# Hybrid encoder layer: the next step's key copies one unit earlier, the output sums behind the first block's low part

## The chip, the cores and the metric

The kernel runs on one core of a Trainium2 chip. Its engines are named as the profile names them: PE is TensorE (PEld is its weight load), DVE is VectorE, ACT is ScalarE, POOL is GpSimd, SP is SyncE, which here only issues DMAs. The metric is the device time of one execution in microseconds (us). Lower is better.

## The reference, cut to what matters

One encoder layer is applied to two sequences of 512 tokens, with model width 1024, all in float32. Attention and a state-space branch read the same normalised input, their gated sum goes through `w_out`, and an MLP follows. The change lies in the attention:

```
s = einsum('nqkgd,njkd->nkgqj', qb, kw) * scale + bias      # query blocks of 128, keys of 3 neighbouring blocks
s = where(mask, s, NEG_INF)
p = softmax(concatenate([s, sink_col]))[..., :-1]
o = einsum('nkgqj,njkd->nqkgd', p, vw)
```

There are 16 query heads of 64, 4 key heads, and 4 query heads share one key head. Queries and keys are RMS-normalised over the 64 elements of a head first. A block of 128 queries sees the key block before it, its own and the one after it, so the first and the last of the four blocks of a sequence see two key blocks and the others three.

## The kernel before, in words

Products are kept close to float32 by splitting operands into a high part (rounded to the matmul's format, made on ACT) and a low part (the rest, made on DVE or POOL).

**Steps and units.** The attention runs over 8 steps (key head j, sequence sq), and each step over 4 units, the query blocks qb = 0 to 3. The order of the work on PE, DVE, ACT and POOL is written out by hand in one loop body, and each engine executes its instructions in that order. SP's queue is ordered by a scheduler. Three things are interleaved in a unit:

- the current block `cur`: `scores(h)` on PE for four heads (L991, into a PSUM tile `sps`, of which there are two), `largest(h)` on DVE (L995, adds the bias and finds the maximum `nmx`; with its accumulator read it frees the `sps` tile), `exp(h)` on ACT (L1001, in place in `p`);
- the block before it, `prev`: `turn(i)` transposes the p of key block i on PE (L1007, into a PSUM tile `tps`, of which there are two), `high(i)` rounds it on ACT (L1011, `ph`), `low(i)` is the rest on DVE (L1016, `pl`), and `value(i, part)` multiplies ph (part 0) or pl (part 1) by the values on PE (L1023). All of a block's value products accumulate in one PSUM tile `po`. The pool of `po` has one buffer, `ps_o` with bufs=1;
- the projection of a query tile of the next step: `project(n)` on PE (L919, `acc`), `square` on ACT (L925, `sq`), `power` on POOL (L932 to L939, `rq`), `norm` on DVE (L943, `qn`), and one unit later `turn` (L952), `high` and `low` (L967, L971, `qa`).

**The output sum.** A value product yields two halves of `po`. At a unit's end ACT copies the lower half (`lower_part`, L1027, `ol`), and in the unit after that DVE adds the two (`owed.add()`, two instructions L1033, each reading `po` and `ol` and writing `ya`). So the sum of block n-2 runs in unit n. In the same unit PE's `value(0, 0)` of block n-1 begins to fill `po` again.

**The key copies.** `key_copies` on POOL (L888) copies the next step's normalised keys twice side by side into `kd`. `key_turn` transposes `kd` on PE (L901, into a `tps` tile), and ACT (L902) and DVE (L903) make `kh` and `kl`, which the next step's scores use. Both happen in the unit qb = 0. `kd` and `qn` share a pool of two buffers.

**Further work.** In units 2 and 3 DVE also multiplies the former step's `ya` by its gate (`late.gated`, L1068) and by the inverse sums (`late.multiply`, L1072). In units 0 and 1 of steps 1 to 4, and in all of steps 0, 6 and 7, ACT and POOL prepare a piece of weights (L873 or L785 on ACT, L874 or L786 on POOL) at a unit's end. Steps 6 and 7 also split the state-space branch's result (L1090 on ACT, L1087 on POOL), and they move the norm into the unit's first half (`prompt`), with a sum over the head on DVE (L936). Step 7 has no next step, so PE fills its gaps with products of the state-space branch (L125).

Lines up to L1180 have the same numbers before and after the change.

Of the kernel before, what the change touches and what calls it, by code (L numbers as in the profile page):

```python
# [33 lines left out]
NB = SEQ // BLOCK  # L34
# [30 lines left out]
def hybrid_layer(ctx, tc, x, x_t, w_kv, rel, onehot, w_qkv, w_ug, vectors, lam, coefs, w_glu, w_out, ln2,  # L65
# [469 lines left out]
    with tc.tile_pool(name="hst", bufs=1) as hp:  # L535
# [11 lines left out]
        with tc.tile_pool(name="ssmt", bufs=2) as sp:  # L547
# [123 lines left out]
            pending = []  # L671
# [166 lines left out]
    with tc.tile_pool(name="att", bufs=2, reuse_waits="tile") as ap, tc.tile_pool(name="attc", bufs=1, reuse_waits="tile") as ac:  # L838
# [17 lines left out]
        steps = [(j, sq) for j in range(N_KV) for sq in range(NSEQ)]  # L856
# [29 lines left out]
        def key_copies(j, sq):  # L886
            kd = ap.tile([P, 4, 2, HD], F32, tag="qn", name="kd")
            GP.tensor_copy(kd, kn[:, sq * 4:sq * 4 + 4, j, None, :].to_broadcast([P, 4, 2, HD]))  # L888
            return kd
# [16 lines left out]
        class Tile:  # L906
# [6 lines left out]
            def project(self, n):  # L913
                (j, sq), col = self.key, self.t * P
                for i in range(self.k, min(self.k + n, 3 * KT)):
                    k, p = divmod(i, 3)
                    hi, lo = weights[j][k // 4]
                    act, w = [(0, hi), (0, lo), (1, hi)][p]
                    PE.matmul(self.ps, hT[sq][act][:, k, col:col + P], w[:, k % 4, :], start=i == 0, stop=i == 3 * KT - 1)  # L919
                self.k += n  # L920
# [186 lines left out]
        def glu_pull(n):  # L1107
            for _ in itertools.islice(early, n):
                pass
# [14 lines left out]
        with tc.manual_schedule(engines={ET.PE, ET.DVE, ET.Activation, ET.Pool}):  # L1124
# [14 lines left out]
            for t in range(4):  # L1139
# [22 lines left out]
                if t == 2:  # L1162
                    kd = key_copies(0, 0)
# [13 lines left out]
                return pending[:2]  # L1177
            return pending[2:]

        pending, y_lows = [], []  # L1180
        prev = owed = lower = turned = None
        with tc.manual_schedule(engines={ET.PE, ET.Activation, ET.DVE, ET.Pool}):
            for i, (j, sq) in enumerate(steps):
                nxt = steps[i + 1] if i + 1 < len(steps) else None
                sums = small.tile([P, G, NB], F32, tag="sm", name="sm", bufs=2)
                ya = ap.tile([P, 2, HALF], F32, tag="ya", name="ya")
                extra = pieces_of(i)
                for qb in range(NB):
                    if 1 <= i < 3:
                        t = (i - 1) * NB + qb  # L1190
                        GP.dma_start(y2_scr[:, :, t, :].rearrange("g c k -> c g k"), y_scr[t])
                    for m in {6: (qb,), 7: ((4, 5, 6, 7), (), (), ())[qb]}.get(i, ()):
                        load_y(m)
                    ready = {6: ((0,), (1,), (2,), (3,)), 7: ((4,), (5, 6), (7,), ())}.get(i, ((),) * 4)[qb]
                    cur = Unit(j, sq, qb, sums, ya)
                    n3 = prev.nkb if prev else 0
                    div = Divide(*steps[i - 1], *done) if qb == 1 and i > 0 else None
                    new = Tile(*nxt, qb) if nxt else None
                    project = new.project if new else lambda n: glu_pull(n // 2)
                    kd, prompt = None, not nxt or (i == 6)  # L1200
                    if rows and not nxt:
                        rows.pt = acc()
                    if rows and not rows.qn:
                        rows.power(halving=not prompt)
                    while y_lows:
                        y_lows.pop(0)()
                    cur.scores(0)
                    cur.largest(0)
                    if i == 7 and qb == 3:
                        final = Divide(j, sq, sums, ya, True)  # L1210
                        final.load_gate(ap, "p", 3)
                    cur.scores(1)
                    if owed:
                        owed.add()
                    cur.largest(1)
                    if n3:
                        prev.turn(0)
                        prev.turn(1)
                        prev.high(0)
                    project(6)  # L1220
                    if n3:
                        prev.low(0)
                    cur.exp(0)
                    cur.exp(1)
                    if rows and not rows.qn and prompt:
                        rows.norm()
                    if qb == 0 and nxt:
                        kd = key_copies(*nxt)
                    if div:
                        div.invert()  # L1230
                    cur.scores(2)
                    cur.largest(2)
                    if n3:
                        prev.high(1)
                    project(4)
                    if n3:
                        prev.value(0, 0)
                    project(2)
                    cur.exp(2)
                    cur.scores(3)  # L1240
                    if lower:
                        lower()
                        lower = None
                    if n3:
                        prev.low(1)
                        prev.value(0, 1)
                    if rows and not rows.qn:
                        rows.norm()
                    cur.largest(3)
                    if n3 > 2:  # L1250
                        prev.turn(2)
                    if rows and prompt:
                        rows.turn()
                    if kd and prompt:
                        key_turn(*nxt, kd)
                    if div:
                        div.turn()
                    project(4)
                    if n3 > 2:
                        prev.high(2)  # L1260
                        prev.low(2)
                    for tile_ in (turned, rows if prompt else None):
                        if tile_:
                            tile_.high()
                            tile_.low()
                    if n3:
                        prev.value(1, 0)
                    if kd and not prompt:
                        key_turn(*nxt, kd)
                    cur.exp(3)  # L1270
                    project(4)
                    if n3:
                        prev.value(1, 1)
                    project(4)
                    turned = None if prompt else rows
                    if turned:
                        rows.turn()
                    if n3 > 2:
                        prev.value(2, 0)
                        prev.value(2, 1)  # L1280
                    if new:
                        new.square()
                    if qb == (2 if nxt else 3) and late:
                        late.gated()
                    if qb == 3 and late and nxt:
                        late.multiply()
                    if n3:
                        prev.lower_part()
                    for m in ready:
                        y_lows += [split_y(m, half) for half in range(2)]  # L1290
                    if extra:
                        lower = extra.pop(0)()
                    if qb == 1:
                        late = div
                    owed, prev, rows = prev, cur, new
                    if nxt and qb == NB - 1 and sq == 1:
                        load_biases(nxt[0])
                done = sums, ya
            owed.add()
            glu_pull(6)  # L1300
            for k in range(prev.nkb):
                prev.turn(k)
                prev.high(k)
                prev.low(k)
                glu_pull(4)
            late.multiply()
            load_gates(0)
            gate_out(0)
            for k in range(prev.nkb):
                prev.value(k, 0)  # L1310
                prev.value(k, 1)
            load_gates(1)
            prev.lower_part()
            prev.add()
            glu_pull(13)
            gate_out(1)
            final.invert()
            final.turn()
            glu_pull(24)
            pieces[2] = glu_pieces(2, cpool, GP)  # L1320
            column_half(2, 0)
            column_half(2, 1)
            final.gated()
            for u in range(2):
                gated_states(u, ap, "qn")
                mixed(u)
            gate_out(2)
            gate_out(3)
            gated_states(2, ap, "qn")
            column_half(3, 0)  # L1330
            column_half(3, 1)
            final.multiply()
# [74 lines left out]
    with tc.tile_pool(name="rn2", bufs=2, reuse_waits="tile") as rn2:  # L1407
# [150 lines left out]
        xb, owed = [], None  # L1558
# [5 lines left out]
        for t in range(NT // 2):  # L1564
# [7 lines left out]
            for sq in range(NSEQ):  # L1572
# [28 lines left out]
                owed = sq, t, norm_of(x1, *scaled)  # L1601
# [280 lines left out]
```

## Time and profile before

| | |
|---|---|
| median of 3 runs | 1445.36 us (1444.78 to 1446.15) |
| the profiled execution | 1444.43 us, of which the span from first to last instruction is 1442.6 us |
| PE busy | 1431.5 us, 99% of the span |
| DVE, ACT, POOL busy | 1097.7, 771.0, 290.6 us |
| granted TensorE clock | 0.999 |
| attention loop | about 432 to 655 us of the span, some 28 us a step |

Busy PE means that matmuls are in flight. Their ends are modelled, and the weight load of the next matmul overlaps the one in flight, so a short stop of PE shows first as idle time ahead of a weight load (PEld). In a row of the timeline stand the start, the duration, the engine, the line, the operation, output<-input and the count; in brackets the idle time ahead of it and what ended it. DVE's next instruction may start a little before the row of the one ahead of it ends.

### The profile page before, as it was taken

The numbers are of one execution on the slowest core, as the hardware profiler recorded it, in microseconds if no ns is written. First come the engines' busy times: TensorE is split into PE (matmuls) and PEld (weight loads), VectorE is DVE, ScalarE is ACT, GpSimd is POOL, SyncE is SP. The second block draws the span as 40 slices with busy tenths as digits, with TensorE's granted clock in tenths as the row PEclk, the third lists the DMA queues.
The fourth block names the chain that finished last, engine by engine and source line by source line (L and its number), as shares of the span: only waits on it lengthen the run. The fifth ranks groups of instructions, "written<-read, shape, count | busy, mean of one in ns | idle before, by whom it ended". The sixth has DMA issues, their size and how long they took to land.

```text
span 1442.6 us, 22132 instructions
## 1 busy us (share of the span) xinstructions
PE 1431.5 (99%) x7941; PEld 1222.5 (85%) x7941; DVE 1097.7 (76%) x1983; ACT 771.0 (53%) x1387; POOL 290.6 (20%) x534
## 2 busy tenths in 40 slices
PE   9999999999999999999999999999999999999998
PEld 7888888889999999887888888888888888888887
DVE  7999959995458999988976588777776597575644
ACT  8688861224348888894543255455544443333332
POOL 3044452004246766463100000000000000000000
PEclk9999999999999999999999999999999999999999
DMA  7356549529641542346552344444442983464341
GB/s 297 102 171 186 177 146 324 206 97 311 224 175 60 166 123 80 119 140 202 182 198 83 132 143 164 161 161 161 147 148 93 364 313 104 147 200 146 120 131 59
DMA packets 102206, 240.24 MB, mean 167 GB/s; under 512 B 12331, under 2 KB 25131, under 8 KB 102097
## 3 DMA queue, kind: packets, MB, share of 16 engines
q1 hardware_dynamic: 62304, 139.94, 29.8%
q0 software_dynamic: 16320, 48.28, 10.1%
q10 hardware_dynamic: 23472, 50.61, 9.5%
q8 instruction: 63, 1.03, 0.3%
q14 instruction: 47, 0.38, 0.1%
HBM read 169.02 MB, written 81.82 MB: 174 GB/s over the span
## 4 chain that ended last, share of the span: by engine, by line
PE 76%; DVE 10%; issue 5%; POOL 3%; ACT 3%; DMA 3%; SPq 0%; DVEq 0%; ACTq 0%; POOLq 0%
PE bank L119 13%; PE bank L120 13%; PE bank L118 13%; PE acc L187 10%; PE acc L125 6%; PE acc L919 3%; PE sps L641 2%; PE sps L753 2%; DVE t L716 2%; PE sps L991 2%; PE acc L120 1%; PE acc L119 1%; PE acc L118 1%; DVE t L718 1%; DVE t L717 1%
## 5 line engine op out<-in xcount | busy, mean ns | idle before, releaser
L187 PE MATMUL acc<-act,c_hi 128*128 128x512 f32 x768 | 243.8, 395 | 0.0
L119 PE MATMUL bank<-b_lo,a_hi 128*128 128x512 f32 (+1 forms) x449 | 174.7, 389 | 0.1
L120 PE MATMUL bank<-b_hi,a_lo 128*128 128x512 f32 (+1 forms) x449 | 174.5, 389 | 0.0
L118 PE MATMUL bank<-b_hi,a_hi 128*128 128x512 f32 (+1 forms) x449 | 174.5, 389 | 0.0
L187 PEld LDWEIGHTS acc<-act,c_hi 128*128 128x128 f32 x768 | 142.3, 188 | 28.0 <-ACT act L316 0.9
L1738 ACT CAST a_hi<-d_a 128x1024 fp32r<-128x1024 f32 x56 | 59.0, 1053 | 178.0 <-PE bank L119 174.7
L187 PE MATMUL acc<-act,c_lo 128*128 128x512 f32 x384 | 151.3, 394 | 0.0
L118 PE MATMUL bank<-act,act 128*128 128x512 f32 x368 | 143.2, 389 | 0.0
L119 PE MATMUL bank<-act,act 128*128 128x512 f32 x368 | 143.2, 389 | 0.0
L120 PE MATMUL bank<-act,act 128*128 128x512 f32 x368 | 143.2, 389 | 0.0
L1739 DVE TENSOR_TENSOR a_lo<-d_a,a_hi 128x1024 fp32r<-128x1024 f32 x56 | 68.5, 1223 | 97.1 <-ACT a_hi L1738 97.1
L919 PE MATMUL acc<-w_hi,act 128*128 128x256 f32 x512 | 113.4, 290 | 0.5 <-DVE qn L943 0.5
L119 PEld LDWEIGHTS bank<-b_lo,a_hi 128*128 128x128 f32 x449 | 84.3, 188 | 18.3 <-DVE b_lo L1739 0.8
L120 PEld LDWEIGHTS bank<-b_hi,a_lo 128*128 128x128 f32 x449 | 84.3, 188 | 17.5
L118 PEld LDWEIGHTS bank<-b_hi,a_hi 128*128 128x128 f32 x449 | 84.3, 188 | 17.4
L919 PEld LDWEIGHTS acc<-w_hi,act 128*128 128x128 f32 x512 | 87.0, 189 | 4.9 <-PE sps L991 0.5
L187 PEld LDWEIGHTS acc<-act,c_lo 128*128 128x128 f32 x384 | 72.2, 188 | 14.6 <-DVE c_lo L178 0.8
L125 PE MATMUL acc<-act,gc_hi 128*128 128x512 f32 x256 | 81.2, 394 | 0.3 <-POOL act L1087 0.3
L119 PEld LDWEIGHTS bank<-act,act 128*128 128x128 f32 x368 | 69.1, 188 | 14.5
L120 PEld LDWEIGHTS bank<-act,act 128*128 128x128 f32 x368 | 69.1, 188 | 14.4
L118 PEld LDWEIGHTS bank<-act,act 128*128 128x128 f32 x368 | 69.1, 188 | 14.2
L1001 ACT ACTIVATE p<-p,nmx 128x257 f32<-128x257 f32 (+1 forms) x128 | 71.8, 563 | 12.9 <-DVE nmx L995 12.0
(370 smaller groups left out, 3467.8 us busy)
## 6 DMA issues: line engine op xcount, KB each, us to landing
d_a<-a_scr SPq DMA_DIRECT2D x56, 512.0 KB, 3.6
raws<-in_w_up_dram SPq DMA_DIRECT2D x32, 512.0 KB, 4.1
a_scr<-t ACTq DMA_DIRECT2D x64, 256.0 KB, 3.0
k<-in_w_down_dram SPq DMA_DIRECT2D x32, 512.0 KB, 6.1
c_raw<-in_w_ug_dram SPq DMA_DIRECT2D x48, 256.0 KB, 3.8
ct_scr<-ctab POOLq DMA_DIRECT2D x16, 512.0 KB, 4.7
ctab_in<-ct_scr POOLq DMA_DIRECT2D x16, 512.0 KB, 6.9
a_scr<-a ACTq DMA_DIRECT2D x32, 256.0 KB, 2.0
```

The source lines that it names most:

```text
L118: PE.matmul(ps, a[0], b[0], start=first, stop=False)
L119: PE.matmul(ps, a[0], b[1], start=False, stop=False)
L120: PE.matmul(ps, a[1], b[0], start=False, stop=last)
L125: PE.matmul(ps, w[wi][:, k, :], rows[yi], start=k + p == 0, stop=k == KT - 1 and p == 2)
L187: PE.matmul(ps, w[wi][:, k, :], hT[s][hi][:, k, :], start=n == 0, stop=n == 3 * KT - 1)
L641: PE.matmul(ps[:, i * P:(i + 1) * P], bm[:, ri, g, :], u_sb[:, gp * SH + g, :], start=True, stop=True)
L716: V.tensor_mul(t1, h[:, i], a8r)
L753: PE.matmul(o, ctab[:, g0 % SI + g, ri, 0:T * CH], st[:, ri, g].rearrange("p s k -> p (s k)"), start=False, stop=ri == 1)
L919: PE.matmul(self.ps, hT[sq][act][:, k, col:col + P], w[:, k % 4, :], start=i == 0, stop=i == 3 * KT - 1)
L1001: S.activation(p, p, AF.Exp, bias=self.nmx[:, h:h + 1], scale=-1.0, accum_out=self.sums[:, h, self.qb:self.qb + 1])
L1738: S.copy(hi, src)
L1739: V.tensor_sub(lo, src, hi.bitcast(F32))
```

## The change

Two edits of the order, no new and no removed instruction. The output sums `owed.add()` move from ahead of `largest(1)` to behind `low(0)` of the block before. The key copies for step i+1, which ran in unit 0 of step i, now run near the end of unit 3 of step i-1, and wait in a list; only the first (made in step 0, for step 1) stays where it was.

```diff
-        pending, y_lows = [], []
+        pending, y_lows, ahead_keys = [], [], []
...
-                    kd, prompt = None, not nxt or (i == 6)
+                    prompt = not nxt or (i == 6)
...
                     cur.scores(1)
-                    if owed:
-                        owed.add()
                     cur.largest(1)
                     if n3:
                         prev.turn(0)
                         prev.turn(1)
                         prev.high(0)
                     project(6)
                     if n3:
                         prev.low(0)
+                    if owed:
+                        owed.add()
                     cur.exp(0)
                     cur.exp(1)
                     if rows and not rows.qn and prompt:
                         rows.norm()
-                    if qb == 0 and nxt:
-                        kd = key_copies(*nxt)
+                    if qb == 0 and i == 0:
+                        ahead_keys.append(key_copies(*nxt))
...
                     if rows and prompt:
                         rows.turn()
+                    kd = ahead_keys.pop() if qb == 0 and nxt else None
                     if kd and prompt:
                         key_turn(*nxt, kd)
...
                     project(4)
+                    if qb == NB - 1 and i + 2 < len(steps):
+                        ahead_keys.append(key_copies(*steps[i + 2]))
                     turned = None if prompt else rows
```

On DVE, in a unit qb = 1 (the instruction that follows is the reciprocal of the sums, L1043), this stood before:

```order
L995 ISA p,nmx<-sps,bias,vec 128x384
L995 ISA nmx 128x1
L1033 TENSOR_TENSOR ya<-po,ol 64x2x128 x2
L995 ISA p,nmx<-sps,bias,vec 128x384
L995 ISA nmx 128x1
L1016 TENSOR_TENSOR pl<-tps,ph 128x512
L1043 RECIPROCAL rsum<-sm 128x16
```

and this stands now:

```order
L995 ISA p,nmx<-sps,bias,vec 128x384
L995 ISA nmx 128x1
L995 ISA p,nmx<-sps,bias,vec 128x384
L995 ISA nmx 128x1
L1016 TENSOR_TENSOR pl<-tps,ph 128x512
L1033 TENSOR_TENSOR ya<-po,ol 64x2x128 x2
L1043 RECIPROCAL rsum<-sm 128x16
```

The two sums moved behind the second `largest` and behind `low(0)`.

On PE nothing moved, but the waits changed. From `value(0, 0)` to `value(0, 1)` of a unit with three key blocks, with the semaphores that each instruction waits for in brackets, before:

```order
L1023 MATMUL po<-ph,va 128x512 [waits DVE_49,Activation_49]
L919 MATMUL acc<-w_lo,act_104 128x256
L919 MATMUL acc<-w_hi,act_105 128x256
L991 MATMUL sps<-kh,qa 128x384 [waits DVE_49]
L991 MATMUL sps<-kl,qa 128x384
L1023 MATMUL po<-pl,va 128x512 [waits DVE_49]
```

and now:

```order
L1023 MATMUL po<-ph,va 128x512 [waits DVE_49,Activation_49]
L919 MATMUL acc<-w_lo,act_104 128x256
L919 MATMUL acc<-w_hi,act_105 128x256
L991 MATMUL sps<-kh,qa 128x384
L991 MATMUL sps<-kl,qa 128x384
L1023 MATMUL po<-pl,va 128x512
```

The waits of `scores(3)` on `largest(1)` and of `value(0, 1)` on `low(0)` are gone: the DVE wait of `value(0, 0)` now covers both.

On POOL, around the start of a step, before:

```order
L939 TENSOR_TENSOR rq<-ms,neg_half 128x4 [waits Pool_49]
L888 COPY kd<-kn 128x512 [waits DVE_49,PE_49]
L1191 DMA y_scr<-y_scr 16x64x128 [waits DMASW5_49]
L983 COPY p<-vec 128x4 [waits DVE_49,PE_49]
L932 TENSOR_TENSOR sq<-sq 128x4x32 [waits Activation_49]
```

and now, one unit earlier:

```order
L939 TENSOR_TENSOR rq<-ms,neg_half 128x4 [waits Pool_49]
L888 COPY kd<-kn 128x512 [waits DVE_49,PE_49]
L1191 DMA y_scr<-y_scr 16x64x128 [waits DMASW4_49]
L983 COPY p<-vec 128x4
L932 TENSOR_TENSOR sq<-sq 128x4x32 [waits Activation_49]
```

The copy moved ahead of one whole chain of `power` (L932 to L939) and of the DMA and the small copy ahead of that chain. On SP one load of the state-space result and the store of a finished `ya` (L1073) change places in step 6, in a queue of which nothing else moves.

## The prediction

> **What bounds the kernel now.** I read the page first, then the stretches of the attention loop and of the stage behind it, then the waits of PE's weight load in the loop.
>
> ```profile
> span 1442.6 us, 22132 instructions
> PE 1431.5 (99%) x7941; PEld 1222.5 (85%) x7941; DVE 1097.7 (76%) x1983; ACT 771.0 (53%) x1387; POOL 290.6 (20%) x534
> ```
>
> ```profile
> 487.00:516.00 29.00, 28.51 (x211) 26.59 (x210) 27.06 (x70) 24.80 (x64) 20.71 (x45) 1.00 0.46 142
> 660.00:680.00 20.00, 20.00 (x90) 16.42 (x90) 18.79 (x24) 7.55 (x14) 5.00 (x5) 1.00 0.65 212
> 720.00:760.00 40.00, 40.00 (x182) 33.19 (x181) 29.39 (x42) 16.89 (x30) 2.68 (x6) 1.00 0.56 195
> ```
>
> ```profile
> PEld po L1023 <- DVE pl L1016: 3.8, 13, 0.3
> PEld tps L901 <- POOL kd L888: 2.5, 4, 0.6
> PEld acc L919 <- POOL w_lo L874: 0.4, 1, 0.4
> ```
>
> PE is the bound: 99% of the span, 28.51 of 29 us in a loop stretch, and all of 20 and 40 us in the stage behind the loop. (Columns of a stretch: its length, PE, PEld, DVE, ACT, POOL busy, the granted clock, DMA.) So a stop taken from PE's order or added to it in the loop passes to the end nearly whole. DVE is close behind in the loop, 27.06 of 29 us. The waits show what the two edits could win at most: 3.8 us for `value` waiting for `pl` (13 times 0.3), 2.5 us for the key transposes waiting for `kd`, 0.4 us for one weight piece behind `kd`.
>
> **The key copies.**
>
> ```profile
> 490.26 0.40 PE L1023 MATMUL po<-ph,va 128*128 128x512 f32 x1
> 490.30 0.60 POOL L888 COPY kd<-kn 128x512 f32<-128x512 f32 x1
> 490.95 0.42 PEld L901 LDWEIGHTS tps<-ident,kd 128*128 128x128 f32 x4 [0.62 <-POOL kd L888]
> 491.37 0.36 PE L919 MATMUL acc<-w_lo,act 128*128 128x256 f32 x1
> 462.28 0.40 PE L1023 MATMUL po<-ph,va 128*128 128x512 f32 x1
> 462.88 0.36 PE L919 MATMUL acc<-w_lo,act 128*128 128x256 f32 x1
> 458.29 1.77 POOL L932 TENSOR_TENSOR sq<-sq 128x128 f32<-128x128 f32 x5 [0.85 <-ACT sq L925]
> ```
>
> From `value(1, 0)` to the projection behind the key transposes PE takes 491.37 - 490.26 = 1.11 us where it waits and 462.88 - 462.28 = 0.60 where it does not: 0.51 us for each of 4 steps, 2.0 us. The copy ends at 490.90 and the load starts at 490.95, so a semaphore costs 0.05. With the weight piece the early copy wins 2.0 + 0.4 = 2.4 us. [...]
>
> Its new place costs nothing: it is 0.60 us of POOL, ahead of the DMA issue and the small copy and one chain of `power`, and there POOL waits for ACT's `sq`, in the tightest case (the first step's end) for 0.85 us. Its inputs and its buffer, last read by the transposes of a query tile at the end of unit 2, are free by then. If that cover were gone, `rq` and `norm` would be late by up to 0.6 us once a step.
>
> **The output sums.** The order alone says that `low(0)` and `largest(1)` come 0.84 us sooner on a busy DVE and that `largest(2)` comes later. But the sums read `po`, `po` has one buffer, and `value(0, 0)` overwrites it. Before, the sums were done long before PE got there. Now they are third behind `largest(0)`. A unit with three key blocks, before:
>
> ```profile
> 492.77 0.42 PE L991 MATMUL sps<-kh,qa 128*128 128x384 f32 x1
> 493.41 0.62 DVE L995 CUSTOM_DVE_ANT_0 p<-sps,bias,vec 128x384 f32<-128x384 f32 x1 [0.27 <-PE sps L991]
> 493.95 0.84 DVE L1033 TENSOR_TENSOR ya<-po,ol 64x256 f32<-64x256 f32 x2
> 494.46 0.58 ACT L1011 CAST ph<-tps 128x512 fp32r<-128x512 f32 x1
> 494.82 0.62 DVE L995 CUSTOM_DVE_ANT_0 p<-sps,bias,vec 128x384 f32<-128x384 f32 x1
> 495.37 0.69 DVE L1016 TENSOR_TENSOR pl<-tps,ph 128x512 fp32r<-128x512 f32 x1
> 495.97 0.40 PE L1023 MATMUL po<-ph,va 128*128 128x512 f32 x1
> 495.97 0.24 DVE L1043 RECIPROCAL rsum<-sm 128x16 f32<-128x16 f32 x1
> ```
>
> DVE waits for PE's first scores, then takes 0.54 us to the next instruction, and `low(0)` takes 0.60 to its next one. After the change the second `largest` ends at 493.41 + 2 x 0.54 = 494.49, but `low(0)` needs `ph`, which ACT ends at 494.46 + 0.58 = 495.04. So `low(0)` starts at 495.07, the sums at 495.67, they end 0.84 later at 496.51, and `value(0, 0)` starts at 496.56 where it started at 495.97. That is 0.59 us of PE standing. In one form for all units: `value(0, 0)` comes 1.52 us after the end of the first `ph` (0.03 + 0.60 + 0.84 + 0.05). Behind PE's stalled instruction stands everything of the unit: projection, `scores(3)`, the other values, the next unit's scores. Nothing of it can pass. DVE's `largest(2)` keeps its distance to `value(0, 0)`, so the unit's tail moves as a whole and gives nothing back.
>
> ```profile
> 445.75 0.59 ACT L1011 CAST ph<-tps 128x512 fp32r<-128x512 f32 x1
> 447.26 0.40 PE L1023 MATMUL po<-ph,va 128*128 128x512 f32 x1
> 556.96 0.59 ACT L1011 CAST ph<-tps 128x512 fp32r<-128x512 f32 x1
> 558.49 0.40 PE L1023 MATMUL po<-ph,va 128*128 128x512 f32 x1
> 578.40 0.59 ACT L1011 CAST ph<-tps 128x512 fp32r<-128x512 f32 x1 [0.28 <-PE tps L1007]
> 580.17 0.40 PE L1023 MATMUL po<-ph,va 128*128 128x512 f32 x1
> ```
>
> *Units in which ACT has a weight cast ahead of `ph`*, 11 of them from 447 to 558: the first gives 446.34 + 1.52 - 447.26 = 0.60, the last 557.55 + 1.52 - 558.49 = 0.58. Nine lie near 0.6 to 0.75, one of step 3 at 0.88; I take 0.65 on average: +7.1 us. *Units 1 and 2 of step 5*, with no cast: 578.99 + 1.52 - 580.17 = 0.34 each: +0.7.
>
> *Unit 3 and the next step's unit 0*, five pairs from 480 to 600. DVE comes late from a 1.2 us multiply:
>
> ```profile
> 485.75 1.22 DVE L1072 TENSOR_TENSOR ya<-ya,fac 128x1024 f32<-128x1024 f32 x1
> 487.01 0.48 DVE L995 CUSTOM_DVE_ANT_0 p<-sps,bias,vec 128x256 f32<-128x256 f32 x1
> 487.42 0.84 DVE L1033 TENSOR_TENSOR ya<-po,ol 64x256 f32<-64x256 f32 x2
> 488.41 0.47 PE L1023 MATMUL po<-ph,va 128*128 128x512 f32 x1
> 489.44 0.19 PEld L1023 LDWEIGHTS po<-pl,va 128*128 128x128 f32 x1 [0.30 <-DVE pl L1016]
> 460.86 0.40 PE L1023 MATMUL po<-ph,va 128*128 128x512 f32 x1
> 461.57 0.40 PE L1023 MATMUL po<-pl,va 128*128 128x512 f32 x1
> ```
>
> Here DVE sets it: 487.01 + 2 x 0.41 + 0.60 + 0.84 + 0.05 = 489.32 against 488.41, +0.91. The wait for `pl` behind it goes, since `low(0)` is now ahead of the sums: `value(0, 1)` follows 1.03 us after `value(0, 0)` where it waits and 0.71 where it does not, so -0.32. Ten units at 0.59: +5.9. In the second of a pair DVE is held by its own queue and not by PE, so part of the first's delay does not come again; DVE's tail of unit 3 moves by about half of it, so I take back 0.3 a pair: -1.5. Ends: 0 and the whole 0.59 (-3.0).
>
> *The last seven units* (step 6 from qb = 1, step 7), where ACT's `ph` itself is late:
>
> ```profile
> 608.99 0.58 ACT L1011 CAST ph<-tps 128x512 fp32r<-128x512 f32 x1
> 609.62 0.50 PE L1023 MATMUL po<-ph,va 128*128 128x512 f32 x1 [0.55 <-ACT ph L1011]
> 649.60 0.59 ACT L1011 CAST ph<-tps 128x512 fp32r<-128x512 f32 x1
> 650.50 0.40 PE L1023 MATMUL po<-ph,va 128*128 128x512 f32 x1
> ```
>
> The form gives 609.57 + 1.52 - 609.62 = 1.47 for the first and 650.19 + 1.52 - 650.50 = 1.21 for the last; the seven lie between 1.0 and 1.5, 8.9 us in all. PE is less the bound here (it waits for ACT in the first row), and ACT and DVE, which run on while PE stands, begin the next unit less late than PE. If all of PE's former lead were eaten first, some 3 us would stay; the form's 8.9 is the other end. I take two thirds, +6.1.
>
> Sum: 7.1 + 0.7 + 5.9 - 1.5 + 6.1 - 2.4 = +15.9 us. The waits for `pl` are lost as intended and cost more than they were worth, because the wait came back one instruction earlier. The profiled execution took 1444.43 us, its span of 1442.6 and 1.8 around it, and lies 0.93 below the median of the runs: 1445.36 + 15.9 = 1461 us.
>
> **The rivals.**
>
> 1. *The sums are hidden.* If `value(0, 0)` reached `po` after the sums anyway, only the gains are left: 3.8 + 2.4 = 6.2 us, so 1439 us. It decides where `value(0, 0)` starts 1.52 us or more behind the end of the first `ph`. In the quoted units it is 0.93 (493), 0.91 (447), 0.94 (557), 1.18 (578). That speaks against it; for it speaks only that a DVE without the sum ahead of `low(0)` also frees `sps` sooner. Chance 4%.
> 2. *It comes to nothing*: stops and gains cancel. The 11 + 2 units would have to cost a third of what the rows give. 4%; 1443 to 1448 us.
> 3. *The loop absorbs half.* DVE and ACT are 93% and 86% busy in the stretch; where they lag PE, PE's stop lets them catch up and later waits vanish. With the low ends everywhere (pairs -3.0, last units +3) and the casts at half, 7.1/2 + 0.7 + 5.9 - 3.0 + 3 - 2.4 = +7.8: 1453 us. 9%.
> 4. *The clock falls.* PE would stand 0.6 us in each 7 us, where it now stands 0.6 in 28 at a granted clock of 1.00. If the clock were halved in one of the eight steps, 28.5 us of busy PE there would take up to 57: 1461 + 28 = 1489 us. [...] 3%.
>
> **How the numbers follow.** The forecast has 80%. A measurement of this kernel can tell about 0.2%, 2.9 us, from no change. Faster has rival 1 (4%), within 0.2% has rival 2 (4%), slower the rest, 92%. The likeliest case alone spans the ends of its terms: the low ends of the pairs and of the last units give 1445.4 + 11.3 = 1456.7, the high ends (no share back, 8.9) 1465.6, and 28 stops that each cost 0.06 more to refill PE, as 0.36 in place of 0.30 would be, 1467. Taken down to the third rival's 1453 and up to 1468 it holds 8 in 10.
>
> **What would show it.** Right: `value(0, 0)` (L1023 on ph) waits for `ya` L1033 on DVE about 28 times, 0.3 to 1.5 us each; the waits of PEld for `kd` and for `pl` at `value(0, 1)` are gone; L888 stands in POOL's gap ahead of `sq`; the loop is some 16 us longer, and the stages behind it keep their lengths. Wrong: no wait for L1033 (then rival 1), or a granted clock below 1.00 in the loop (rival 4), or new waits for `nmx` on ACT that end in `turn(0)` waiting for `p`, which would add to the forecast.

## The result, and the profile after

The changed kernel takes 1469.62 us in the median (1468.10 to 1470.52, 5 runs), the kernel before 1445.36 (1444.78 to 1446.15, 5 runs): a ratio of 1.0167, 95% interval 1.0152 to 1.0182. It is slower by 24 us. The prediction was slower, with 1461 us and a range up to 1468, so the direction and the place were right and the size was 8.6 us short. The profiled execution took 1468.10 us.

The head of the page after, and the same kind of stretches as before (length; PE, PEld, DVE, ACT, POOL busy; granted clock; DMA):

```profile
span 1466.3 us, 22121 instructions
PE 1433.1 (98%) x7941; PEld 1223.2 (83%) x7941; DVE 1097.8 (75%) x1983; ACT 771.6 (53%) x1387; POOL 290.9 (20%) x534
```

```profile
489.00:519.00 30.00, 27.20 (x201) 25.35 (x200) 25.91 (x65) 24.18 (x62) 20.40 (x44) 1.00 0.50 155
720.00:760.00 40.00, 40.00 (x178) 33.15 (x177) 38.20 (x56) 21.60 (x38) 3.17 (x6) 1.00 0.56 184
```

No engine does more work than before: busy times agree within 2 us. In a loop stretch PE now stands 2.80 of 30 us where it stood 0.49 of 29. Behind the loop it is still busy all of 40 us. The waits in the loop, after:

```profile
PE po L1023 <- DVE ya L1033: 24.7, 30, 2.1
ACT p L1001 <- DVE nmx L995: 22.8, 41, 1.0
DVE pl L1016 <- ACT ph L1011: 21.8, 37, 1.3
PEld po L1023 <- ACT ph L1011: 16.5, 15, 1.6
PEld po L1023 <- ACT p L1001: 14.4, 15, 2.3
```

The new wait is the first row: 30 products `value(0, 0)` wait for the sums. The two PEld rows are the same 30 stops seen by the weight load, and they name ACT. That is the row to distrust: the load waits for DVE and for ACT, and ACT's `ph` was long done. The unit that the prediction worked through (before: 492.77 to 495.97), after:

```profile
500.16 0.59 ACT L1011 CAST ph<-tps 128x512 fp32r<-128x512 f32 x1
500.78 0.69 DVE L1016 TENSOR_TENSOR pl<-tps,ph 128x512 fp32r<-128x512 f32 x1 [0.50 <-ACT ph L1011]
501.38 0.84 DVE L1033 TENSOR_TENSOR ya<-po,ol 64x256 f32<-64x256 f32 x2
502.34 0.19 PEld L1023 LDWEIGHTS po<-ph,va 128*128 128x128 f32 x1 [0.69 <-ACT p L1001]
502.37 0.47 PE L1023 MATMUL po<-ph,va 128*128 128x512 f32 x1 [0.51 <-DVE ya L1033]
502.68 0.28 PE L919 MATMUL acc<-w_lo,act 128*128 128x256 f32 x1
```

`ph` ends at 500.75, `low(0)` starts 0.03 later, the sums 0.60 later and take 0.84, all as the form had it. Then it parts from the form: the load starts 0.12 behind the sums' end (the form had 0.05 to the product), the product 0.03 later, and PE's next product 0.31 after that. Before, with PE running, that last distance was 0.23:

```profile
495.97 0.40 PE L1023 MATMUL po<-ph,va 128*128 128x512 f32 x1
496.20 0.28 PE L919 MATMUL acc<-w_lo,act 128*128 128x256 f32 x1
```

So this stop costs 0.10 + 0.08 = 0.18 us more than the form says: the way from DVE to the load of a stalled PE, and the longer distance to the next product, called the refill from here on. The first part is the same in all 30 stops (the product starts 0.14 to 0.16 us behind the sums' end). The refill is new in 17 of them only. In the ten units of the pairs and in the first three of the last seven, PE had stood at this place before the change too, and its next product followed 0.30 to 0.34 us behind then, and 0.30 to 0.31 now. A unit of a pair, the first two rows before (the product itself at 488.41, quoted in the prediction), the others after:

```profile
488.71 0.28 PE L919 MATMUL acc<-w_lo,act 128*128 128x256 f32 x1
489.44 0.50 PE L1023 MATMUL po<-pl,va 128*128 128x512 f32 x1
494.99 0.47 PE L1023 MATMUL po<-ph,va 128*128 128x512 f32 x1 [0.88 <-DVE ya L1033]
495.30 0.28 PE L919 MATMUL acc<-w_lo,act 128*128 128x256 f32 x1
495.77 0.40 PE L1023 MATMUL po<-pl,va 128*128 128x512 f32 x1
```

DVE now idles 0.50 us ahead of `low(0)`, where it used to do the sums for nothing.

### The profile page after: what moved, and what is told of

Its sections match the earlier page's. It is cut to its first block, busy times and chain, and to the rows that moved or that the text cites. A ratio compares the mean times of both kernels' runs of the same rounds, so it can differ in the third digit from the quotient of the medians.

```text
span 1466.3 us, 22121 instructions
## 1 busy us (share of the span) xinstructions
PE 1433.1 (98%) x7941; PEld 1223.2 (83%) x7941; DVE 1097.8 (75%) x1983; ACT 771.6 (53%) x1387; POOL 290.9 (20%) x534
## 4 chain that ended last, share of the span: by engine, by line
PE 76%; DVE 11%; issue 5%; ACT 4%; DMA 2%; POOL 1%; DVEq 0%; ACTq 0%; SPq 0%; POOLq 0%
PE bank L119 13%; PE bank L120 13%; PE bank L118 13%; PE acc L187 10%; PE acc L125 6%; PE acc L919 3%; PE po L1023 2%; PE sps L641 2%; PE sps L753 2%; DMA c_raw<-in_w_ug_dram 1%; DVE ya L1033 1%; PE acc L120 1%; PE acc L118 1%; PE acc L119 1%; DVE t L716 1%
```

## The experiments

All ratios are to the kernel before on the same chip. In what follows "the shift" of a unit is how much later its products start than in the profile before.

**One edit at a time.** Key copies alone: the changed kernel with `owed.add()` back ahead of `largest(1)`.

```diff
                     cur.scores(1)
+                    if owed:
+                        owed.add()
                     cur.largest(1)
...
                         prev.low(0)
-                    if owed:
-                        owed.add()
```

> The key copies early, the output sums in their old place. Theory (the whole loss is PE's wait for the sums in front of value(0, 0)): 2.4 to 2.6 us faster than before, 1442.8 to 1443.0, and no wait for ya. Rival (the early copies themselves disturb POOL's chain of power or PE's projection): 1445 or more.

1443.10 us, ratio 0.9979 (0.9970 to 0.9988): the gain is there, 3.0 us by the ratio. The waits for `kd` and `w_lo` are gone, that for `pl` stays:

```profile
PEld po L1023 <- DVE pl L1016: 3.8, 13, 0.3
```

The sums alone (the second edit on the kernel before):

> The output sums behind low(0), the key copies in their old place. Theory: the stops of the whole change stay and the 2.4 to 2.6 us of the key copies come back on top, 1472 us. If the wait for kd were already covered by the stop of PE ahead of it, 1469.6 as with both.

1470.62 us, ratio 1.0167 (1.0153 to 1.0180), the same as with both edits. The second case holds: PE's stop in unit 0 covers the late copy. In this kernel, at the start of a step:

```profile
495.62 0.60 POOL L888 COPY kd<-kn 128x512 f32<-128x512 f32 x1
496.21 0.39 PE L1023 MATMUL po<-ph,va 128*128 128x512 f32 x1
496.27 0.53 PEld L901 LDWEIGHTS tps<-ident,kd 128*128 128x128 f32 x4
```

The load for the key transposes no longer waits at all, though the copy ends only 0.05 ahead of it. The early copies are worth 3 us alone and nothing that can be measured beside the stops.

**Is it `po`, or DVE's order?** First try: the sums read `ol` twice.

```diff
-                    V.tensor_add(self.ya[...], pov[:, :, e], olv[:, :, e])
+                    V.tensor_add(self.ya[...], olv[:, :, e], olv[:, :, e])
```

> The changed kernel, but the sums read ol twice in place of po and ol, so that nothing in PE's way depends on them (the output leaves out po's upper half). DVE's order is that of the changed kernel. Theory (one buffer of po): no stop ahead of value(0, 0), and the waits for pl and kd are gone as well, 1439 to 1441 us. Rival (DVE's new order itself, with largest(2) and what follows it later): 1455 or more.

1459.55 us, ratio 1.0095 (1.0081 to 1.0108): by these numbers the rival. But the trace shows that the edit brought something of its own. Up to the end of step 5 the shift grows by only 0.9 us; the loss sits in steps 6 and 7, where the sums, now with both operands in SBUF, take up to 2.65 us beside POOL's work:

```profile
612.47 2.65 DVE L1033 TENSOR_TENSOR ya<-ol 64x256 f32<-64x256 f32 x2
613.40 1.44 POOL L786 TENSOR_TENSOR gc_lo<-c_raw,gc_hi 128x512 fp32r<-128x512 f32 x1
615.16 0.42 DVE L943 TENSOR_TENSOR qn<-acc,rq 128x256 f32<-128x256 f32 x1
615.63 0.63 PE L949 MATMUL acc<-ident,qn 128*64 128x128 f32 x4 [2.42 <-DVE qn L943]
```

With `po` as an operand a pair of sums took 0.83 to 0.85 everywhere in the profiles before and after, also beside POOL's L1087 on 128x512 (0.84 at 642.17 in the profile after, where L1087 runs from 641.64 to 644.15). The slow sums of `ol` stand beside POOL's instructions on 128x512; in steps 1 to 5, beside POOL's small ones, the sums of `ol` took 0.84 to 0.89 too. Why they are slow there was not shown. `norm` stands behind the sums and PE behind `norm`. A part of this loss is the granted clock (below). The run answers another question than the one asked, so it was done again with an operand from PSUM that PE does not write next: the tile that `low(0)` has just read.

```diff
-                        owed.add()
+                        owed.add(prev.pt[0])
```

> The changed kernel, but the sums read the transposed p of the block before (the PSUM tile that low(0) has just read) in place of po, so that PE's value(0, 0) does not depend on them and DVE's instructions keep their order, their operand from PSUM and their 0.84 us (the output leaves out po's upper half). Theory (one buffer of po): 1439 to 1443 us, with the loop within 2 us of the one with the key copies alone. Rival (the order of DVE costs it even where PE need not wait, and the run with the sums from ol alone was slow for that): 1455 us or more.

1446.42 us, ratio 1.0003 (0.9994 to 1.0011). The theory holds in the main: with the dependence on `po` gone, 23 of the 24 us are gone. It does not hold within its 1439 to 1443: this is 3.3 us above the key copies alone, with the same gain in `kd`. The waits say where:

```profile
PEld tps L1007 <- PE sps L991: 4.4, 13, 0.6
PEld sps L991 <- DVE nmx L995: 4.3, 13, 0.7
PEld po L1023 <- DVE pl L1016: 0.4, 2, 0.2
```

The wait for `pl` is gone (3.8 to 0.4), as rival 1 wanted. In its place PE waits for `nmx` (4.3 us, 13 times; 1.3 us, 3 times before) and ahead of `turn(2)`, 4.4 us. The latter comes from this experiment's own operand, since `turn(2)` now has to wait until the sums have read the tile (its load starts 0.12 us behind the sums' end there). How much of the 3.3 us DVE's order alone would cost is therefore bounded, not settled. In this run the intended gain of the second edit is not there; without the 4.4 us of its own it would be at most about 1 us (1446.4 - 4.4 = 1442.0 against 1443.1), which no run here shows.

**Give PE work ahead of the wait.** `value(0, 0)` goes directly ahead of `value(0, 1)`, the rest as changed.

```diff
                     project(4)
-                    if n3:
-                        prev.value(0, 0)
                     project(2)
                     cur.exp(2)
                     cur.scores(3)
...
                         prev.low(1)
+                        prev.value(0, 0)
                         prev.value(0, 1)
```

> The changed kernel with value(0, 0) moved behind project(2), exp(2) and scores(3), directly ahead of value(0, 1): PE gets 0.48 us of other work ahead of the wait (0.71 from value to value, less 0.23 of the first one). Theory: a stop of 0.78 in the units with a cast goes down to 0.3, those of unit 3 and unit 0 to 0.3 to 0.5, those of the last seven units to some 0.7, which is some 14 us of the 24, so 1453 to 1458 us. Rival (DVE's order costs it, wherever PE waits): 1465 or more.

1452.88 us, ratio 1.0053 (1.0041 to 1.0066), 17 us back with no change on DVE:

```profile
PE po L1023 <- DVE ya L1033: 10.9, 23, 1.5
```

The stops fell by 13.8 us, 0.46 for each of 30, seven are gone with their refill, and the mean clock is 1.000 in all five executions (the longest stop left is 1.55 us by PE's idle time, 1.84 by the weight load's). The time lies just under the theory's range. What counts is when PE reaches the wait.

**The three classes of units, each alone**, with the key copies early throughout (base: 1443.10 us, ratio 0.9979) and the sums behind `low(0)` in one class of units, elsewhere ahead of `largest(1)`. For the pairs:

```diff
                     cur.scores(1)
+                    if owed and not (i * NB + qb in (7, 8, 11, 12, 15, 16, 19, 20, 23, 24)):
+                        owed.add()
                     cur.largest(1)
...
                         prev.low(0)
-                    if owed:
+                    if owed and (i * NB + qb in (7, 8, 11, 12, 15, 16, 19, 20, 23, 24)):
                         owed.add()
```

> Key copies early; the sums behind low(0) only in the 13 units in which ACT's weight cast is ahead of ph or DVE is on time (units 2 to 6, 9, 10, 13, 14, 17, 18, 21, 22 of 32), elsewhere in their old place. By the prediction's form (7.1 + 0.7 on top of 1443.1 with the key copies alone): 1450.9. If each stop costs 0.17 to 0.19 more than the form, as the profile after has it (0.78 a unit with a cast, 0.52 in the two without): +9.9, so 1453.0 us.

> Key copies early; the sums behind low(0) only in the ten units of the pairs (unit 3 of a step and unit 0 of the next, 7 to 24). By the prediction's terms (5.9 less 1.5 for the carry, on top of 1443.1): 1447.5. If each stop costs as the profile after has it (0.66 and 0.59 at the unit's end): +6.2, so 1449.3 us.

> Key copies early; the sums behind low(0) only in the last seven units (step 6 from its second unit, step 7). By the prediction's two thirds of the form (6.1): 1449.2. By the profile after, whose clock stayed at 1.00: +8.2, so 1451.3. If the mean clock falls to 0.997 to 0.998 here, as in the other executions of the changed kernel, some 1.5 to 3 us on top: 1453 to 1454 us, and then the clock of the two runs with the other units is 0.999 to 1.000.

| units | median us | ratio (95%) | cost over the key copies alone | predicted | with 0.17 a stop more |
|---|---|---|---|---|---|
| cast and step 5 (13) | 1452.79 | 1.0047 (1.0035 to 1.0059) | 9.8 | 7.8 | 10.0 |
| pairs (10) | 1449.09 | 1.0022 (1.0013 to 1.0031) | 6.2 | 4.4 | 6.1 |
| last seven | 1453.19 | 1.0052 (1.0039 to 1.0064) | 10.5 | 6.1 | 7.3 |

(The cost is the difference of the ratios times 1445.4 and is uncertain by some 2 us.) The units with a cast and those of step 5 come out at the form plus 0.17 us for each stop, 0.10 to the product and 0.07 in the refill. The pairs do so only in the sum: their units have no new refill, and the carry that the 4.4 counts on is not there. DVE around the first pair, the first row before, the others in the run with the pairs alone:

```profile
478.50 1.23 DVE L1068 TENSOR_TENSOR ya<-ya,gate 128x1024 f32<-128x1024 f32 x1
479.61 1.23 DVE L1068 TENSOR_TENSOR ya<-ya,gate 128x1024 f32<-128x1024 f32 x1
485.60 0.69 DVE L1016 TENSOR_TENSOR pl<-tps,ph 128x512 fp32r<-128x512 f32 x1 [0.54 <-ACT ph L1011]
487.45 1.23 DVE L1072 TENSOR_TENSOR ya<-ya,fac 128x1024 f32<-128x1024 f32 x1
```

Ahead of the pair DVE is 1.11 us behind the profile before; at L1072, which stood at 485.75, it is 1.70 behind. DVE's tail of unit 3 moved by 0.59, the whole delay of PE and not half of it, since DVE too waited there (for `ph`). So the second unit of a pair pays as much as the first: against the key copies alone, PE falls back by 0.59 to 0.61 us in the first unit of the five pairs and by 0.59 to 0.67 in the second.

The parts add up: 9.8 + 6.2 + 10.5 - 3.0 = 23.5 us, against 24.1 for the whole. The last seven units cost 3 us more than the form plus 0.17 a stop (at the full clock of the profile after they cost 8.2).

**The clock.** Those 3 us led to the granted clock. Of the changed kernel's five executions, the profiled one has a mean clock of 1.000, the other four 0.997 to 0.998, and these took 1.1 to 2.4 us longer. In the run with the last seven units alone, the profile caught it: one stop, then four stretches of 2 us:

```profile
609.64 0.47 PE L1023 MATMUL po<-ph,va 128*128 128x512 f32 x1 [2.13 <-DVE ya L1033]
```

```profile
608.00:610.00 2.00, 0.36 (x2) 0.35 (x3) 1.91 (x5) 1.69 (x6) 2.00 (x3) 1.00 0.00 0
610.00:612.00 2.00, 2.00 (x10) 1.56 (x9) 1.69 (x6) 0.71 (x2) 0.99 (x2) 0.57 0.09 8
612.00:614.00 2.00, 2.00 (x11) 1.90 (x10) 0.67 (x1) 1.44 (x4) 0.00 (x0) 0.58 0.42 127
614.00:616.00 2.00, 2.00 (x16) 1.92 (x16) 0.62 (x3) 0.94 (x3) 0.03 (x1) 1.00 0.18 31
```

Half clock throughout would read 0.50, so the missing 0.43 and 0.42 of two stretches of 2 us are (0.43 + 0.42) x 2 / 0.5 = 3.4 us at half clock, right behind a stop of 2.13 us (from 610.50 to 613.50 the clock reads 0.50). The next unit's products then come 3.10 us later than in the profile before, where at full clock (the profile after) they lose 1.55 us. In the profile after, the stop of the same unit was as long, and the clock stayed whole:

```profile
626.07 0.19 PEld L1023 LDWEIGHTS po<-ph,va 128*128 128x128 f32 x1 [2.31 <-ACT p L1001]
```

```profile
626.00:628.00 2.00, 1.90 (x13) 1.74 (x14) 2.00 (x6) 0.88 (x4) 1.46 (x3) 1.00 0.00 0
```

So it happens in some executions and not in others. Three more profiles show it. With the sums alone the clock fell behind both long stops (2.15 and 1.77 us of PE), and each of the two units lost 3.1 to 3.2 us; with the first two products exchanged (below) it fell behind the second (1.76 us) only. In the first try with `ol` the stops were ahead of L949 and not at `po`, 2.42 and 2.02 us, and behind them:

```profile
616.00:620.00 4.00, 4.00 (x21) 3.78 (x19) 2.22 (x7) 2.58 (x8) 0.00 (x0) 0.60 0.22 67
628.00:632.00 4.00, 4.00 (x23) 3.78 (x22) 3.83 (x9) 2.72 (x8) 0.58 (x2) 0.69 0.02 6
```

(With the 0.97 and 0.88 of the two stretches between, some 3.4 us of that loop's loss are the clock's.) The two longest stops, in the second and third unit of step 6, were then taken away alone (sums in their old place in these two units).

> The changed kernel with the sums back in their old place in two units alone, the second and third of step 6, whose stops were the longest (2.3 and 1.95 us). Theory (a stop of about 2 us makes the clock fall to half for some 3.4 us in part of the executions, and that is why most executions of the changed kernel show a mean clock of 0.997 to 0.998): the two stops' 1.55 + 1.53 = 3.1 us go, and 1.5 us of lost clock with them, 1465.0 us, and every execution shows 0.999 to 1.000. Rival (the low clock has nothing to do with these two stops): 1466.5 us, with the mean clock still at 0.997 to 0.998 in most executions.

1464.64 us, ratio 1.0134 (1.0117 to 1.0151), and all four executions at a clock of 1.000. The time is the theory's, but its interval (1462 to 1467) holds the rival's 1466.5 too; what speaks for the theory is the clock. The longest stops left are 1.55 us by the weight load's idle time, 1.15 by PE's:

```profile
648.15 0.19 PEld L1023 LDWEIGHTS po<-ph,va 128*128 128x128 f32 x1 [1.55 <-ACT ph L1011]
```

**Two semaphores or one?** The first two products of a block exchanged, so that `pl` comes first (and carries the start of the accumulation).

```diff
-                        prev.value(0, 0)
+                        prev.value(0, 1)
...
-                        prev.value(0, 1)
+                        prev.value(0, 0)
```

> The changed kernel with the first two value products of a block exchanged: the product with pl (made on DVE) stands where value(0, 0) stood, the product with ph (made on ACT) where value(0, 1) stood. The first of them then waits on DVE alone and not on DVE and ACT. Theory (a weight load that has to wait on two semaphores starts 0.11 to 0.12 us after the sums, on one 0.05): the product comes 0.06 sooner behind the sums in each of 30 units, 1.8 us in all, 1467.8 us, and the refill of PE behind it stays at 0.30. Rival (0.11 is what any stop costs): the distance stays at 0.11 to 0.12, and the time at 1469.6 us.

1469.81 us, ratio 1.0163 (1.0149 to 1.0177), unchanged, and so is the chain:

```profile
508.57 0.84 DVE L1033 TENSOR_TENSOR ya<-po,ol 64x256 f32<-64x256 f32 x2
509.52 0.19 PEld L1023 LDWEIGHTS po<-pl,va 128*128 128x128 f32 x1 [0.72 <-ACT p L1001]
509.55 0.47 PE L1023 MATMUL po<-pl,va 128*128 128x512 f32 x1 [0.54 <-DVE ya L1033]
```

The sums end at 509.41 and the load starts 0.11 later. This decides nothing: the product that is now first still waits for ACT too, since ACT has read `po` in `lower_part`. Whether the second semaphore or the kind of DVE instruction makes 0.11 of what is 0.05 behind `pl` stays open.

**A version that beats both?** The key copies alone are the best here. One more step was tried on it: PE work where it waits for `pl`.

```diff
                     cur.scores(3)
+                    project(2)
...
                         div.turn()
-                    project(4)
+                    project(2)
```

> The kernel with the key copies early and the sums in their old place, with two of the four projection products that follow the transposes of the third key block put ahead of value(0, 1), so that PE has 0.23 us of work where it waits 0.3 us for pl in 13 units. Theory (PE's order passes to the end whole): 13 x 0.23 = 3.0 us off 1443.1 to 1443.4, so 1440.3 us; what remains of the wait for pl is under 1 us. Rival (turn(2) and what follows it come 0.23 later in all units, and ACT's ph or DVE's later work becomes late instead): 1443 us or more.

1443.62 us, ratio 0.9983 (0.9974 to 0.9992): no gain over 0.9979. The rival has the time, and the waits show a mechanism near it:

```profile
PEld po L1023 <- DVE pl L1016: 0.4, 2, 0.2
PEld sps L991 <- DVE nmx L995: 3.7, 14, 0.7
```

```profile
516.42 0.19 PEld L991 LDWEIGHTS sps<-kh,qa 128*128 128x128 f32 x1 [0.24 <-DVE nmx L995]
```

Of the 3.4 us that left the wait for `pl`, 2.4 came back as waits of the scores for `nmx` (3.7 us, 1.3 before). These waits say that in units 3 and 0 DVE's queue sets the pace, so that PE waits for it at one place or at the next. The 3.8 us that stood in the waits for `pl` were not to be had by this reordering of PE; no other was tried.

## Why the prediction was right or wrong

- *The key copies, -2.4.* Right alone: 3.0 us by the ratio, 2.6 in the loop of the profile. Not foreseen: beside the stops they bring nothing, since a stop in unit 0 covers the late copy (the sums alone cost as much as both edits).
- *The sums: the wait, its place and its chain.* Right: 30 waits of `value(0, 0)` for L1033 (its text says 28, its terms count 30 units), and `value(0, 0)` at the form's time but for a constant. Taking the dependence on `po` away brought 23 us back.
- *The form's constant failed, and this is the largest part of the miss.* The step took "a semaphore costs 0.05" from POOL's copy and applied it to DVE's sums and a stalled PE, and left the refill to the range's upper end as "28 stops that each cost 0.06 more". Measured: 0.15 from the sums' end to the product, 0.10 more than the form, in 30 stops, and 0.07 in the refill of the 17 stops where PE had not stood before: 3.0 + 1.2 = 4.2 us. The cast units and step 5 taken alone confirm it (9.8 us, where the form with both gives 10.0). Why it is 0.15 here and 0.05 there stays open.
- *The pairs' carry, -1.5.* Wrong, and hidden by the number. Its step was that DVE's tail of unit 3 moves by about half of PE's delay; it moved by 0.59 of 0.60. The pairs alone cost 6.2 us, which is the form's 5.9 without any carry, nearly unchanged. The product does come 0.10 later than the form has it (1.00 for 0.91), but some 0.4 comes back behind it, where the form counted 0.32 for the wait for `pl`. That 4.4 and 0.17 a stop give 6.1 is luck.
- *The last seven units: "I take two thirds".* Too little. In the profile after they cost 8.2 us. The form's 8.9 with 0.10 a stop and the refills would be 9.8, so 1.6 came back where the prediction took back 3.0: PE's lead was eaten less than assumed. That is 1.2 us beyond restart and refill.
- *Rival 4, the clock.* Its form was wrong and its kind was right. The prediction bound it to a whole step at half clock (+28 us) and gave it 3%. No run shows a step at half clock. What happened is small: by the mean clocks one or two drops of 3.4 us in most executions, behind stops of about 2 us. Taking the two stops away brought 4.8 us by the ratios, of which the stops themselves are 3.1, so some 1.7 us are the clock's. (The ratios are uncertain by some 2 us; the four executions at the lower clock took 1.1 to 2.4 us longer than the one at 1.000.)
- *Rivals 1 and 3.* Rival 1's condition (PE reaching `po` late) was brought about by the run with another operand, and even then its 1439 did not come: 1446.4, of which up to 4.4 are that run's own wait. Rival 3's absorption by half was not seen: no class of units cost less than its term.
- In the profiled execution the loop grew by 21.8 us, 5.9 above the forecast 15.9: restart and refill 4.2, the last seven 1.2, the pairs 0.4 (beyond their restart). A further 1.4 us lies ahead of the loop, where nothing was changed. Such a shift also shows with the key copies alone (1.9 us), in the slowest execution (1445.25 us) of a kernel whose median is 1443.10, so it is scatter. Of the median's 8.6 us, 4.2 + 1.2 + 0.4 + 1.7 = 7.5 are accounted for; the rest, about 1 us, is within the scatter.

## What to carry to other kernels

A read that is moved later also moves the write that must wait for it: before moving work on a less loaded engine, look for the next writer of each buffer it reads, and ask when the bounding engine gets there. Price a new stop of that engine from its own restart, measured where it already stops (here 0.10 us to the product and, where it had been running, 0.07 in the refill), not from another engine's semaphore; over thirty small stops that came to 4 of the 24 us. A term that comes out right in the sum can still be wrong, as the pairs' carry was: look at the rows on which its step rests. And a wait that PE has for a busy engine is only a gain if that engine has slack: otherwise, as with `pl` and `nmx` (2.4 of 3.4 us), it returns at the next place.

## What the hardware showed that was not expected

- The granted clock fell to half for some 3.4 us behind PE stops of 1.76 to 2.42 us in four profiles, and not behind other such stops: in the profile after, 2.14 and 1.77 us left it whole. With no stop over 1.55 us (`value(0, 0)` behind `scores(3)`) the mean clock stayed at 1.000 in all five executions. What decides whether a stop brings the drop was not shown.
- A pair of sums with two SBUF operands took 2.65 us beside POOL's instructions on 128x512 and 0.84 to 0.89 beside its small ones. With one operand in PSUM it took 0.83 to 0.85 everywhere in the profiles before and after.
- In the wait views, a load that waits for two engines was put down to ACT 30 times, while the matmul's own row named DVE, which the chain of times bears out.
